# S5 tiles in a pool that gives way to gelu's, gelu in two halves, S5 transfers on POOL's queue: one change to a hybrid decoder layer

## The chip, the cores and the metric

One core of one Trainium2 chip. The metric is device time in microseconds of one execution.

## The reference, cut to what matters

A layer takes 320 token columns (256 of a prompt, 8 samples of 8) of width 2048. One projection feeds a convolution module and an S5 state-space layer; both are joined by an output projection, then come a SwiGLU FFN and a norm. All is fp32.

```python
def s5_mixer(u, h_re, h_im, A_re, A_im, log_dt, B_re, B_im, C_re, C_im, D, w_glu):
    ...
    bu_re = jnp.einsum('blgc,gpc->blgp', uf, Bb_re)
    bu_im = jnp.einsum('blgc,gpc->blgp', uf, Bb_im)
    ...
    _, _, hs_re, hs_im = lax.associative_scan(_complex_scan_op, (a_re, a_im, bu_re, bu_im), axis=1)
    y = (jnp.einsum('blgp,gcp->blgc', hs_re, C_re.astype(f32))
         - jnp.einsum('blgp,gcp->blgc', hs_im, C_im.astype(f32)))
    y = y + D.astype(f32).reshape(N_SSM_GROUPS, SSM_GROUP_CH) * uf
    y = jax.nn.gelu(y.reshape(b, l, D_SSM))
    y = y * jax.nn.sigmoid(y @ w_glu.astype(f32))
```

## The kernel before, in words

The weight matrices are read in slots: a slot is one raw tile of two blocks of 128 input rows by 512 columns (`run_slot`, L131). Its load is issued on SP's queue nine slots ahead (L116); ScalarE writes the high part hi (L126) and VectorE the rest lo (L127), two slots ahead; TensorE runs three products for each 128x128 block (L150 to L152). Every engine works through its own instructions strictly in order, and so does each queue of transfers, so a lo part that stands behind a waiting VectorE instruction holds up TensorE. The slots go: two groups for the S5 input (8 slots each), four for the convolution, then w_glu, w_out and the FFN (from about 450 us to the end).

Beside the projection's slots the S5 work is strewn in by the table PLAN (L31 to L45) and P_POST, P_CONV and P_GELU: each entry is a job and a slot number, its priority, from which a scheduler fixes the order in each engine's queue. There are eight blocks of 128 S5 channels. For each: `pool_v` (L602, tiles vw) and `pool_w` (L613, ww) multiply powers of the state matrix with B and C on VectorE; `s5_cblk` and `s5_pre` (L624, L631) make the kernel matrix ks; `kt_out` (L745) transposes it, adds D on a diagonal (dbc is D spread over the partitions by a transfer, dm that times a mask) and writes kt to KTd in DRAM (L756); `s_in_evac` (L656) puts the projected input into s_in and, after four blocks, sends it by eight transfers to ud in DRAM (L667) and by four back into us (L669); `s5_e`, `s5_scan` and `post` (L672, L703, L1154) make the states and the output yd, for which `make_t` (L758) reads tst from KTd. CT holds C transposed: its lower 64 partitions are written by ScalarE (L578), its upper 64 come from a tile up by a transfer (L582). `gelu` (L812) loads yd back as yl (L818, sixteen transfers) and needs the tiles ge and gehl, which lie where the pool s5 was; `open_g` (L794) closes that pool first. The convolution's `conv_chunk` (L342) fills ubuf (L361), spreads it by four transfers into ub (L371) and multiplies (L379). All of these transfers are on SP's queue.

```python
    def sm_tile(shape, name):
        return s5.tile(shape, F32, name=name, tag="sm", bufs=4)
```

dbc, dm, ks and kt share these four buffers.

Of the kernel before, what the change touches and what calls it, by code (L numbers as in the profile page):

```python
# [55 lines left out]
def kernel(ctx: ExitStack, tc: tile.TileContext,  # L56
# [208 lines left out]
    def channel_vectors():  # L265
        with when(13):
            p = sx_tile([128, 56])
            T.transpose(p, pvn, ident[:56, :56])
            V.tensor_copy(PV[:, 16:72], p)
            for h in range(2):  # L270
                ps = sx_tile([128, 4, 31])
                for c in range(4):
                    T.transpose(ps[:, c, :], late["cwn"][:31, (4 * h + c) * 128:(4 * h + c + 1) * 128],
                                ident[:31, :31])
                V.tensor_copy(convw[:, 4 * h:4 * h + 4, 0:31], ps)
# [10 lines left out]
    def rstd_bcast(dst, v):  # L286
# [3 lines left out]
        ps = sx_tile([128, NTOK])  # L290
        for j, (t0, n, _) in enumerate(tok):
            T.matmul(ps[:, t0:t0 + n], g[:n, j:j + 1].to_broadcast([n, 128]), ident[:n, :n],
                     start=True, stop=True)
        V.tensor_copy(dst, ps)
# [935 lines left out]
```

## Time and profile before

| what | us |
|---|---|
| median of 3 runs | 1442.85 (1442.59 to 1447.15) |
| profiled execution, its own time | 1442.68 |
| span of the profile | 1440.9 |
| TensorE busy | 1390.1 (96%) |
| VectorE busy | 793.9 (55%) |
| ScalarE busy | 550.2 (38%) |
| GpSimd (POOL) busy | 2.2 (17 instructions) |

The profile is one execution; the span leaves out a little at its ends. The page's chain that ended last is 84% TensorE, 6% transfers and 4% SP's queue. In the rows below PE is TensorE, DVE VectorE, ACT ScalarE, SP the queue of SyncE that issues transfers (SPq).

### The profile page before, as it was taken

How to read it: one execution, taken by the hardware profiler on the slowest of the kernel's cores; microseconds unless marked ns; L12 is line 12 of the kernel's file. 1: busy time of each engine (PE TensorE's matmuls, PEld its weight loads, DVE VectorE, ACT ScalarE, POOL GpSimd, SP SyncE). 2: the span in 40 equal slices, each digit the busy share in tenths (PEclk: the TensorE clock that was granted, in tenths of full speed). 3: DMA queues.
4: the chain of work that ended last, by engine and by line, in shares of the span. 5: the costliest groups of instructions: out<-in, count | busy, mean ns of one | idle time of the engine just before them, and what ended most of it. 6: DMA issues, size and time to landing. Idle time of an engine off the chain costs nothing.

```text
span 1440.9 us, 25146 instructions
## 1 busy us (share of the span) xinstructions
PE 1390.1 (96%) x10433; PEld 1358.5 (94%) x10433; DVE 793.9 (55%) x1408; ACT 550.2 (38%) x804; POOL 2.2 (0%) x17
## 2 busy tenths in 40 slices
PE   8899998989998999999999999999999999999995
PEld 7798978878998999999999999999999999999995
DVE  6677995354887845434544444344445444444465
ACT  7334433353454533333333332233333323333232
POOL 0000000000000000000000000000000000000000
PEclk9999998999999999999999999999999999999998
DMA  9775565596343444444444444444444454454432
GB/s 264 209 157 157 156 161 163 137 252 181 132 140 110 157 144 151 147 149 152 151 150 147 148 158 148 147 147 155 152 146 148 147 160 147 147 181 154 148 132 73
DMA packets 165579, 223.51 MB, mean 155 GB/s; under 512 B 40945, under 2 KB 77097, under 8 KB 165320
## 3 DMA queue, kind: packets, MB, share of 16 engines
q1 hardware_dynamic: 165464, 221.90, 50.9%
q8 instruction: 82, 1.34, 0.4%
q14 instruction: 33, 0.27, 0.1%
HBM read 201.56 MB, written 10.41 MB: 147 GB/s over the span
## 4 chain that ended last, share of the span: by engine, by line
PE 84%; DMA 6%; SPq 4%; DVE 3%; ACT 1%; issue 1%; ACTq 0%; DVEq 0%
PE mm L151 26%; PE mm L150 26%; PE mm L152 26%; DMA ub<-ubuf 2%; PE cx L379 2%; SPq L371 1%; SPq L667 1%; DMA raw<-in_w_in_dram 1%; DMA cn<-in_ssm_C_im_dram 1%; DVE lo L127 1%; PE sx L784 1%; DMA h<-xTd 1%; DMA ud<-s_in 0%; SPq L818 0%; PE sx L680 0%
## 5 line engine op out<-in xcount | busy, mean ns | idle before, releaser
L127 DVE TENSOR_TENSOR lo<-raw,hi 128x1024 fp32r<-128x1024 f32 x352 | 430.6, 1224 | 448.6 <-ACT hi L126 446.1
L126 ACT ACTIVATE hi<-raw 128x1024 fp32r<-128x1024 f32 x352 | 372.8, 1060 | 649.4 <-PE mm L151 580.7
L150 PE MATMUL mm<-hn,hi 128*128 128x320 f32 x1408 | 434.8, 309 | 0.0
L151 PE MATMUL mm<-hn,hi 128*128 128x320 f32 x1408 | 434.7, 309 | 0.0
L152 PE MATMUL mm<-hn,lo 128*128 128x320 f32 x1408 | 431.1, 309 | 0.0
L150 PEld LDWEIGHTS mm<-hn,hi 128*128 128x128 f32 x1408 | 264.3, 188 | 0.1
L151 PEld LDWEIGHTS mm<-hn,hi 128*128 128x128 f32 x1408 | 264.3, 188 | 0.0
L152 PEld LDWEIGHTS mm<-hn,lo 128*128 128x128 f32 x1408 | 263.2, 188 | 0.0
L150 PE MATMUL mm<-aout,hi 128*128 128x320 f32 x704 | 217.4, 309 | 0.0
L151 PE MATMUL mm<-aout,hi 128*128 128x320 f32 x704 | 217.1, 309 | 0.0
L152 PE MATMUL mm<-aout,lo 128*128 128x320 f32 x704 | 214.7, 309 | 0.0
L151 PEld LDWEIGHTS mm<-aout,hi 128*128 128x128 f32 x704 | 132.2, 188 | 0.0
L150 PEld LDWEIGHTS mm<-aout,hi 128*128 128x128 f32 x704 | 132.2, 188 | 0.0
L152 PEld LDWEIGHTS mm<-aout,lo 128*128 128x128 f32 x704 | 131.5, 188 | 0.0
L152 PE MATMUL mm<-xhl,lo 128*128 128x320 f32 x384 | 120.3, 318 | 5.7 <-DVE lo L127 5.7
L151 PE MATMUL mm<-xhl,hi 128*128 128x320 f32 x384 | 122.6, 321 | 0.5 <-DVE xhl L254 0.5
L150 PE MATMUL mm<-xhl,hi 128*128 128x320 f32 x384 | 118.0, 321 | 0.2 <-ACT xhl L253 0.2
L152 PEld LDWEIGHTS mm<-xhl,lo 128*128 128x128 f32 x384 | 73.8, 193 | 6.4 <-DVE lo L127 6.0
L151 PEld LDWEIGHTS mm<-xhl,hi 128*128 128x128 f32 x384 | 74.2, 193 | 1.9 <-DVE xhl L254 0.7
L150 PEld LDWEIGHTS mm<-xhl,hi 128*128 128x128 f32 x384 | 72.7, 193 | 1.6 <-issue 1.0
L1048 DVE TENSOR_TENSOR h<-mm,h 128x320 f32<-128x320 f32 x64 | 30.0, 488 | 41.1 <-PE mm L152 41.1
L379 PE MATMUL cx<-ub,cw 128*32 128x256 f32 x512 | 36.3, 391 | 9.4 <-DMA ub<-ubuf 9.4
(306 smaller groups left out, 1322.7 us busy)
## 6 DMA issues: line engine op xcount, KB each, us to landing
raw<-in_w_ffn_gate_dram SPq DMA_DIRECT2D x88, 512.0 KB
raw<-in_w_ffn_up_dram SPq DMA_DIRECT2D x88, 512.0 KB
raw<-in_w_ffn_down_dram SPq DMA_DIRECT2D x88, 512.0 KB
raw<-in_w_in_dram SPq DMA_DIRECT2D x64, 256.0 KB
raw<-in_w_out_dram SPq DMA_DIRECT2D x32, 512.0 KB
ub<-ubuf SPq DMA_DIRECT2D x32, 316.0 KB
raw<-in_w_in_dram SPq DMA_DIRECT2D x16, 512.0 KB
tst<-KTd SPq DMA_DIRECT2D x8, 512.0 KB
```

What stands on the lines that cost most here:

```text
L126: A.activation(hi, src, AF.Copy)
L127: V.tensor_tensor(lo, src, hi.bitcast(F32), op=OP.subtract)
L150: T.matmul(ps, wh, xh, start=(k == 0), stop=False)
L151: T.matmul(ps, wh, xl, start=False, stop=False)
L152: T.matmul(ps, wl, xh, start=False, stop=(k == g.nk - 1))
L371: SP.dma_start(ub[:, b, :], bass.AP(tensor=u.tensor, offset=u[32 * b:32 * b + 32].offset, ap=[[u.ap[0][0], 32], [8, 4], [1, UW - 24]]))
L379: T.matmul(acc[32 * b:32 * b + 32, 0:256], cw[:, b, k, :], ub[:, b, k:k + 256], start=(k == 0), stop=False, skip_group_check=True)
L667: SP.dma_start(o[g], s_in[16 * g:16 * g + 16].rearrange("c m s j -> c (m s) j"))
L784: T.matmul(ps[:, g, :], t2[:, g].rearrange("p t c -> p (t c)"), uall[:, 8 * b + g, :], start=False, stop=(g == 7), skip_group_check=True)
L1048: V.tensor_tensor(h[:, n, :], ps, h[:, n, :], op=OP.add)
```

## The change

It has five parts. (1) The tiles that the first half of the S5 work uses (s_in, cblk, vw, et, prm, tb, braw, cn0) lie in a pool s5v of their own; `open_ge` closes it early, and ge and yl take its place. (2) gelu's jobs are split: blocks 0 to 3 come four slots after the fourth post, blocks 4 to 7 after the last one, and the hi/lo parts are made by a job of their own, `gelu_parts`; one ScalarE step of gelu is folded into a VectorE one. P_POST moves by up to two slots. (3) CT's upper half is written directly: 32 matmuls to 64 rows in place of 16 transposes, and no transfer; cn1 has a buffer of its own. (4) D enters ks on VectorE by a constant matrix e7 and a column of the parameter table PV; dbc and dm are gone, and ks and kt alone share the four sm buffers. (5) The transfers to and from ud, KTd, and xTd into h are issued by GpSimd (`G.dma_start`). Small moves: the zero fill of KTd is one transfer, the parameter rows load earlier, and the conv taps have a function of their own.

```diff
--- before.py
+++ after.py
@@ -20,9 +20,8 @@
-P_POST = [24, 25.5, 27, 28.5, 30, 31.5, 33, 34.5]
+P_POST = [26 + 1.5 * b for b in range(8)]
...
-P_GELU = 44
@@ -38,8 +37,12 @@
+        + [("open_ge", 0, S1 + 4.5)]
+        + [("gelu", b, P_POST[3] + 4 + b) for b in range(4)]
...
-        + [("gelu", b, P_GELU + b / 2) for b in range(8)]
+        + [("gelu2", b, P_POST[7] + 1.2 + 0.1 * b) for b in range(4)]
+        + [x for b in range(4, 8) for x in (("gelu", b, P_POST[7] + 2 + 0.5 * b),
+                                            ("gelu2", b, P_POST[7] + 2.1 + 0.5 * b))]
@@ -159,10 +162,11 @@
-    dmask = const.tile([128, 16], F32, name="dmask")
+    dmask = tmp.tile([128, 8, 16], F32, tag="t", name="dmask")
...
-    V.tensor_scalar(dmask, im, 112.0, None, op0=OP.is_equal)
+    V.tensor_scalar(dmask, im[:, None, :].to_broadcast([128, 8, 16]), 112.0, None, op0=OP.is_equal)
+    e7 = const.tile([128, 128], F32, name="e7")
@@ -179,27 +183,29 @@
-               (gnorm_conv, 8), (gnorm_ssm, 8)]
-    PV = const.tile([128, 72], F32, name="PV")
+               (gnorm_conv, 8), (gnorm_ssm, 8), (ssm_D, 8)]
+    PV = const.tile([128, 80], F32, name="PV")
...
     def pv(i):
...
-    NMIX, NFFN, CB, LNG, LNB, GNC, GNS = 0, 16, 32, 40, 48, 56, 64
+    NMIX, NFFN, CB, LNG, LNB, GNC, GNS, SSD = 0, 16, 32, 40, 48, 56, 64, 72
...
+    vpool = ctx.enter_context(ExitStack())
+    s5v = vpool.enter_context(tc.tile_pool(name="s5v", bufs=1, side="right"))
...
     def sm_tile(shape, name):
...
-    pvn = tmp.tile([56, 128], F32, tag="t", name="pvn")
+    pvn = tmp.tile([64, 128], F32, tag="t", name="pvn")
@@ -229,6 +235,8 @@
+
+    def load_taps():
@@ -263,16 +271,20 @@
     def channel_vectors():
...
+        p = sx_tile([128, 64])
+        T.transpose(p, pvn, ident[:64, :64])
+        V.tensor_copy(PV[:, 16:80], p)
+        p = sx_tile([128, 128])
+        T.transpose(p, dmask.rearrange("p g c -> p (g c)"), ident)
+        A.activation(e7, p, AF.Copy)
+
+    def tap_vectors():
...
@@ -406,10 +419,10 @@
-    s_in = s5.tile([128, 4, 8, 41], F32, name="s_in")
+    s_in = s5v.tile([128, 4, 8, 41], F32, name="s_in")
...
-    Cblk = [s5.tile([128, 4, 2, 2, 16], F32, name=f"cblk{i}") for i in range(N_CBLK)]
+    Cblk = [s5v.tile([128, 4, 2, 2, 16], F32, name=f"cblk{i}") for i in range(N_CBLK)]
     def cmul(eng, outr, outi, ar, ai, br, bi, t1, t2):
@@ -441,8 +454,9 @@
     def s5_load2():
-        braw = s5.tile([128, 2, 32, 16], F32, tag="et", name="braw", bufs=ET)
-        cn = [s5.tile([128, 8, 64], F32, name=f"cn{i}", tag="et", bufs=ET) for i in range(2)]
+        braw = s5v.tile([128, 2, 32, 16], F32, tag="et", name="braw", bufs=ET)
+        cn = [s5v.tile([128, 8, 64], F32, name="cn0", tag="et", bufs=ET),
+              s5.tile([128, 8, 64], F32, name="cn1", tag="ww", bufs=VW)]
@@ -556,30 +570,31 @@
         G.memset(hbd, 0.0)
-        for b in range(8):
-            SP.dma_start(KTd[b, 8:15], z)
+        SP.dma_start(KTd[:, 8:15].rearrange("b s c n -> (s c) b n"),
+                     z[:, None, :].to_broadcast([112, 8, 128]))
...
         kib = kim[:, :, None].to_broadcast([128, 32, 16])
-        tb = s5.tile([128, 2, 512], F32, name="tb", tag="vw", bufs=VW)
+        tb = s5v.tile([128, 2, 512], F32, name="tb", tag="vw", bufs=VW)
...
-        up = s5.tile([64, 2, 32, 16], F32, name="up", tag="ww", bufs=VW)
...
             for h in range(2):
-                ps = sx_tile([64, 4, 128])
+                ps = sx_tile([128, 4, 128])
                 for k in range(4):
-                    T.transpose(ps[:, k, :], cn[r][:, 4 * h + k, :], ident)
-                for g2, dst in enumerate((CT[:64], up)):
-                    A.activation(dst[:, r, 16 * h:16 * h + 16, :]
+                    for g2 in range(2):
+                        T.matmul(ps[64 * g2:64 * g2 + 64, k, :], cn[r][:, 4 * h + k, :], ident,
+                                 start=True, stop=True)
+                for g2 in range(2):
+                    sl = slice(64 * g2, 64 * g2 + 64)
+                    A.activation(CT[sl, r, 16 * h:16 * h + 16, :]
                                  .rearrange("p (k q) c -> p k q c", k=4),
-                                 ps.rearrange("p k (q g c) -> p k q g c", q=4, g=2)[:, :, :, g2, :],
+                                 ps[sl].rearrange("p k (q g c) -> p k q g c", q=4, g=2)[:, :, :, g2, :],
                                  AF.Copy, scale=-1.0 if r else 1.0)
-        SP.dma_start(CT[64:128], up)
@@ -650,7 +665,7 @@
-        A.activation(ks, ps, AF.Copy)
+        V.scalar_tensor_tensor(ks, e7, pv(SSD + b), ps, op0=OP.mult, op1=OP.add)
...
     def s_in_evac(b, ps):
@@ -664,9 +679,9 @@
         for g in range(8):
-            SP.dma_start(o[g], s_in[16 * g:16 * g + 16].rearrange("c m s j -> c (m s) j"))
+            G.dma_start(o[g], s_in[16 * g:16 * g + 16].rearrange("c m s j -> c (m s) j"))
         for m in range(b - 3, b + 1):
-            SP.dma_start(uall[:, 8 * m:8 * m + 8, :].rearrange("p g j -> p (g j)"),
+            G.dma_start(uall[:, 8 * m:8 * m + 8, :].rearrange("p g j -> p (g j)"),
...
     def s5_e(b):
@@ -743,21 +758,15 @@
     def kt_out(b, ks):
-        dbc = sm_tile([128, 128], "dbc")
-        SP.dma_start(dbc, bass.AP(tensor=ssm_D.tensor, offset=ssm_D.offset + 128 * b,
-                                  ap=[[0, 128], [1, 128]]))
-        dm = sm_tile([128, 8, 16], "dm")
-        V.tensor_tensor(dm, dbc.rearrange("p (g c) -> p g c", g=8),
-                        dmask[:, None, :].to_broadcast([128, 8, 16]), op=OP.mult)
...
         kt = sm_tile([128, 128], "kt")
-        V.tensor_tensor(kt, ps, dm.rearrange("p g c -> p (g c)"), op=OP.add)
-        SP.dma_start(KTd[b, 0:8], kt)
+        A.activation(kt, ps, AF.Copy)
+        G.dma_start(KTd[b, 0:8], kt)
     def make_t(b):
         ts_ = s5.tile([128, 8, 8, 16], F32, name="tst", tag="tst", bufs=1)
-        SP.dma_start(ts_, bass.AP(tensor=KTd.tensor, offset=KTd.offset + b * 15 * 2048,
+        G.dma_start(ts_, bass.AP(tensor=KTd.tensor, offset=KTd.offset + b * 15 * 2048,
@@ -791,12 +800,17 @@
+    def open_ge():
+        vpool.close()
+        gst = cpool.enter_context(ExitStack())
+        late["gep"] = gst.enter_context(tc.tile_pool(name="gep", bufs=1, side="right"))
+        late["ge"] = late["gep"].tile([128, 8, NTOK], F32, name="ge")
+
     def open_g():
...
-        late["ge"] = gp.tile([128, 8, NTOK], F32, name="ge")
...
     def open_mid():
@@ -810,23 +824,27 @@
     def gelu(b):
-        gp = late["gp"]
-        ge, gehl = late["ge"], late["gehl"]
+
+        gep, ge = late["gep"], late["ge"]
         if b % 4 == 0:
-            yls = late["yl"] = gp.tile([128, 32, 40], F32, name="yl", bufs=2)
+            yls = late["yl"] = gep.tile([128, 32, 40], F32, name="yl", bufs=2)
...
         yl = late["yl"][:, 8 * (b % 4):8 * (b % 4) + 8]
-        sq = gp.tile([128, 8, 40], F32, name="gsq", bufs=3)
-        A.activation(sq, yl, AF.Square)
-        A.activation(sq, sq, AF.Copy, bias=C0, scale=C0 * 0.044715)
-        z = gp.tile([128, 8, 40], F32, name="gz", bufs=3)
-        V.tensor_tensor(z, sq, yl, op=OP.mult)
-        A.activation(z, z, AF.Sigmoid)
+        if b < 4:
+            z = s5.tile([128, 8, 40], F32, name="gz", tag="pt1", bufs=PT_BUFS)
+        else:
+            z = late["gp"].tile([128, 8, 40], F32, name="gz", bufs=3)
+        A.activation(z, yl, AF.Square)
+        V.scalar_tensor_tensor(z, z, 1.0 / 0.044715, yl, op0=OP.add, op1=OP.mult)
+        A.activation(z, z, AF.Sigmoid, scale=C0 * 0.044715)
...
         V.tensor_tensor(gv, z, yl, op=OP.mult)
+
+    def gelu_parts(b):
+        ge, gehl = late["ge"], late["gehl"]
@@ -945,8 +963,8 @@
-            A.activation(h[:, k, 0:1], late["ge"][:, 4, 0:1], AF.Copy)
-            SP.dma_start(h[:, k:k + 4, :], xTd[:, k:k + 4, :])
+            A.activation(h[:, k, 0:1], late["ssm"][:, 0, 7 if k else 3, 0:1].bitcast(F32), AF.Copy)
+            G.dma_start(h[:, k:k + 4, :], xTd[:, k:k + 4, :])
     def m1_done(i, R):
         def f(m, ps):
@@ -1124,6 +1142,7 @@
+        load_params()
@@ -1135,8 +1154,11 @@
-        load_params()
-    channel_vectors()
+        load_taps()
+    with when(2):
+        channel_vectors()
+    with when(13):
+        tap_vectors()
@@ -1157,9 +1179,9 @@
-    parts_ = dict(v=pool_v, pre=pre, e=s5_e, w=pool_w, scan=s5_scan, post=post, gelu=gelu,
+    parts_ = dict(v=pool_v, pre=pre, e=s5_e, w=pool_w, scan=s5_scan, post=post, gelu=gelu, gelu2=gelu_parts,
...
-                  states=lambda b: s5_states(), open_g=lambda b: open_g(),
+                  states=lambda b: s5_states(), open_g=lambda b: open_g(), open_ge=lambda b: open_ge(),
...
```

**SP's queue where the first S5 input is sent.** Names are tile<-source; raw is a weight load. Before:

```order
L116 DMA raw<-in_w_in_dram 128x2x512
L233 DMA cwn<-in_conv_w_dram 31x1024
L667 DMA ud<-s_in 16x32x41 x8
L582 DMA CT<-up 64x1024
L116 DMA raw<-in_w_in_dram 128x2x512
L669 DMA us<-ud 128x328 x4
L116 DMA raw<-in_w_in_dram 128x2x512
L116 DMA raw<-in_w_in_dram 128x2x256 x8
L336 DMA tapd<-convw 128x8x32
L337 DMA tapw<-tapd 128x32x8
L116 DMA raw<-in_w_in_dram 128x2x256 x3
```

The change:

```order
L119 DMA raw<-in_w_in_dram 128x2x512 x3
L119 DMA raw<-in_w_in_dram 128x2x256 x8
L349 DMA tapd<-convw 128x8x32
L119 DMA raw<-in_w_in_dram 128x2x256 x2
L350 DMA tapw<-tapd 128x32x8
L119 DMA raw<-in_w_in_dram 128x2x256 x38
```

The eight ud, four us, CT and dbc rows are no longer between the weight loads.

**POOL's queue, the change.** Before it held no transfer.

```order
L682 DMA ud<-s_in 16x32x41 x8
L684 DMA us<-ud 128x328 x4
L765 DMA KTd<-kt 128x128
L682 DMA ud<-s_in 16x32x41 x8
L765 DMA KTd<-kt 128x128
L684 DMA us<-ud 128x328 x4
L765 DMA KTd<-kt 128x128 x3
L769 DMA tst<-KTd 128x8x128
L765 DMA KTd<-kt 128x128
L769 DMA tst<-KTd 128x8x128
L765 DMA KTd<-kt 128x128 x2
L769 DMA tst<-KTd 128x8x128 x6
```

The KTd row of block 1 stands behind the second eight ud rows, each tst row behind the KTd rows ahead of it.

**SP's queue around gelu's loads.** so and uo are outputs, stn the convolution's old state. Before:

```order
L818 DMA yl<-yd 16x32x40
L116 DMA raw<-in_w_glu_dram 128x2x512
L818 DMA yl<-yd 16x32x40 x6
L116 DMA raw<-in_w_glu_dram 128x2x512
L818 DMA yl<-yd 16x32x40 x9
L353 DMA stn<-in_state_conv_dram 120x2x128
L371 DMA ub<-ubuf_110 128x1x632 x4
```

The change, the first eight yl rows:

```order
L832 DMA yl<-yd 16x32x40 x3
L384 DMA ub<-ubuf_114 128x1x632 x4
L832 DMA yl<-yd 16x32x40
L799 DMA yd<-y_2682 128x320
L379 DMA out_dram<-uo 30x128
L380 DMA out_dram<-uo 8x8x128
L119 DMA raw<-in_w_in_dram 128x2x256 x2
L832 DMA yl<-yd 16x32x40 x4
```

And the second eight:

```order
L832 DMA yl<-yd 16x32x40
L747 DMA out_dram<-so_3142 32x128
L747 DMA out_dram<-so_3147 32x128
L832 DMA yl<-yd 16x32x40 x5
L119 DMA raw<-in_w_in_dram 128x2x256 x2
L756 DMA out_dram<-so_3154 8x16x128
L832 DMA yl<-yd 16x32x40 x2
L756 DMA out_dram<-so_3161 8x16x128
```

Eight of the sixteen now stand behind the yd row of block 3, among the S5 outputs; the other eight stand among the state outputs, and the next chunk's stn and ub come behind them.

## Rows read from the trace of the kernel before

**Rows 1.** Windows: time; busy of PE, PEld, DVE, ACT, POOL; PEclk; DMA; GB/s.
```profile
60.00:120.00 60.00, 51.26 (x361) 48.44 (x360) 37.46 (x74) 19.73 (x30) 0.00 (x0) 0.91 0.79 172
...
280.00:360.00 80.00, 68.94 (x940) 62.49 (x940) 41.20 (x64) 36.26 (x79) 0.00 (x0) 0.98 0.84 216
...
450.00:1400.00 950.00, 950.00 (x6480) 949.75 (x6480) 456.31 (x596) 336.61 (x393) 0.00 (x0) 1.00 0.47 150
```

**Rows 2.** Windows of 20 us, same columns.
```profile
60.00:80.00 20.00, 14.26 (x80) 12.95 (x79) 10.13 (x29) 4.86 (x6) 0.00 (x0) 0.83 0.82 198
100.00:120.00 20.00, 17.01 (x132) 16.14 (x131) 11.04 (x17) 7.46 (x13) 0.00 (x0) 0.91 0.98 195
...
280.00:300.00 20.00, 14.42 (x185) 12.88 (x185) 7.35 (x11) 7.70 (x19) 0.00 (x0) 0.91 1.07 183
```

**Rows 3.** Waits of TensorE, 0 to 500 us: total us, times, longest.
```profile
PE cx L379 <- DMA ub<-ubuf: 9.4, 8, 2.0
PE mm L152 <- DVE lo L127: 6.7, 2, 5.7
PE sx L363 <- ACT ubuf L361: 4.8, 1, 4.8
PE sx L650 <- DVE kt L755: 3.0, 1, 3.0
...
PE sx L576 <- DMA cn<-in_ssm_C_im_dram: 1.4, 1, 1.4
```

**Rows 4.** Timeline of VectorE: start, us, instruction, idle before and releaser.
```profile
70.67 0.69 DVE L595 TENSOR_TENSOR ww<-pw,CT 128x512 f32<-128x512 f32 x1 [9.87 <-DMA CT<-up]
...
111.02 0.29 DVE L750 TENSOR_TENSOR dm<-dbc,dmask 128x128 f32<-128x128 f32 x1 [6.32 <-DMA dbc<-in_ssm_D_dram]
```

**Rows 5.** Timeline of SP's queue, 44 to 76 us: start, us, issue.
```profile
53.55 11.44 SPq L667 DMA_DIRECT2D ud<-s_in  x8
65.09 0.63 SPq L582 DMA_DIRECT2D CT<-up  x1
```

**Rows 6.** Timeline of SP's queue, 90 to 135 us.
```profile
95.55 4.17 SPq L667 DMA_DIRECT2D ud<-s_in  x6
99.82 0.65 SPq L756 DMA_DIRECT2D KTd<-kt  x1
...
106.86 0.35 SPq L747 DMA_DIRECT2D dbc<-in_ssm_D_dram  x1
...
130.15 0.34 SPq L756 DMA_DIRECT2D KTd<-kt  x1
```

**Rows 7.** Timeline of SP's queue, 276 to 300 us.
```profile
281.81 6.33 SPq L818 DMA_DIRECT2D yl<-yd  x6
...
288.72 6.03 SPq L818 DMA_DIRECT2D yl<-yd  x9
```

**Rows 8.** Timeline of ScalarE, 280 to 300 us.
```profile
293.79 0.47 ACT L823 ACTIVATE gsq<-yl 128x320 f32<-128x320 f32 x1 [7.75 <-DMA yl<-yd]
294.17 0.35 ACT L361 ACTIVATE ubuf<-sx 128x240 f32<-128x240 f32 x1
```

**Rows 9.** Groups of TensorE by shape, 40 to 130 us: busy us, mean ns.
```profile
L650 PE MATMUL sx<-vw,cblk 128*32 128x128 f32 x64 | 2.7, 279 | 3.0 <-DVE kt L755 3.0
L576 PE MATMUL sx<-ident,cn 128*64 128x128 f32 x16 | 2.2, 272 | 1.4 <-DMA cn<-in_ssm_C_im_dram 1.4
```

**Rows 10.** Single lines, L667 and L760: ns min/median/max, first and last start.
```profile
L667 SPq DMA_DIRECT2D ud<-s_in x16: 331/770/4909, 53.6 to 101.9; - x16
...
L760 SPq DMA_DIRECT2D tst<-KTd x8: 360/368/1667, 153.7 to 245.8; - x8
```

**Rows 11.** Groups of VectorE, 45 to 125 us: busy us, mean ns, idle before.
```profile
L275 DVE COPY convw<-sx 128x124 f32<-128x124 f32 x2 | 0.6, 286 | 0.4 <-PE sx L273 0.4
```

More of the change, by code (lines that the diff above doesn't have):

```diff
@@ L257, in x_block @@
                 nc.any.tensor_copy(xr, ps)
-            with when(k):
+            with when(k / 2 - 1):
                 SP.dma_start(xTd[:, k, :], xr)
@@ L265, in channel_vectors @@
     def channel_vectors():
[L266 to L275, printed above, removed]
+        p = sx_tile([128, 64])
[5 more added lines that the diff above has]
+    def tap_vectors():
+        for h in range(2):
+            ps = sx_tile([128, 4, 31])
+            for c in range(4):
+                T.transpose(ps[:, c, :], late["cwn"][:31, (4 * h + c) * 128:(4 * h + c + 1) * 128],
+                            ident[:31, :31])
+            V.tensor_copy(convw[:, 4 * h:4 * h + 4, 0:31], ps)
     def newton_rsqrt(dst, v, t):
@@ L284, in newton_rsqrt, with rstd_bcast @@
             V.scalar_tensor_tensor(dst, t, 1.5, dst, op0=OP.add, op1=OP.mult)
-    def rstd_bcast(dst, v):
+    def rstd_bcast(dst, v, later=0):
         g, t = (tmp.tile([128, 3], F32, name=n, tag="rt", bufs=4) for n in ("rg", "rt"))
         newton_rsqrt(g, v, t)
[L290 to L294, printed above, removed]
+        with when((tc.cur_priority - BASE) / SLOT + later):
+            ps = sx_tile([128, NTOK])
+            for j, (t0, n, _) in enumerate(tok):
+                T.matmul(ps[:, t0:t0 + n], g[:n, j:j + 1].to_broadcast([n, 128]), ident[:n, :n],
+                         start=True, stop=True)
+            V.tensor_copy(dst, ps)
     def token_mean(src, n_ch):
@@ L466, in s5_params @@
             T.transpose(ps[:, i, :], dtn if i == 2 else an[i], ident[:32, :32])
-        prm = s5.tile([128, 1024], F32, name="prm", tag="vw", bufs=VW)
+        prm = s5v.tile([128, 1024], F32, name="prm", tag="vw", bufs=VW)
         P = s5p["P"] = prm[:, 0:512].rearrange("p (i q) -> p i q", q=32)
@@ L569, in s5_params2 @@
         cmul(V, Bb[:, 0], Bb[:, 1], krb, kib, braw[:, 0], braw[:, 1], tb0, tb1)
-        up = s5.tile([64, 2, 32, 16], F32, name="up", tag="ww", bufs=VW)
         for r in range(2):
             for h in range(2):
-                ps = sx_tile([64, 4, 128])
+                ps = sx_tile([128, 4, 128])
                 for k in range(4):
-                    T.transpose(ps[:, k, :], cn[r][:, 4 * h + k, :], ident)
-                for g2, dst in enumerate((CT[:64], up)):
-                    A.activation(dst[:, r, 16 * h:16 * h + 16, :]
+                    for g2 in range(2):
+                        T.matmul(ps[64 * g2:64 * g2 + 64, k, :], cn[r][:, 4 * h + k, :], ident,
+                                 start=True, stop=True)
+                for g2 in range(2):
+                    sl = slice(64 * g2, 64 * g2 + 64)
+                    A.activation(CT[sl, r, 16 * h:16 * h + 16, :]
                                  .rearrange("p (k q) c -> p k q c", k=4),
-                                 ps.rearrange("p k (q g c) -> p k q g c", q=4, g=2)[:, :, :, g2, :],
+                                 ps[sl].rearrange("p k (q g c) -> p k q g c", q=4, g=2)[:, :, :, g2, :],
                                  AF.Copy, scale=-1.0 if r else 1.0)
-        SP.dma_start(CT[64:128], up)
         for r in range(2):
@@ L602, in pool_v @@
     def pool_v(b):
-        v = s5.tile([128, 4, 2, 8, 16], F32, name="vw", tag="vw", bufs=VW)
+        v = s5v.tile([128, 4, 2, 8, 16], F32, name="vw", tag="vw", bufs=VW)
         Vt[b] = v
@@ L637, in s5_pre @@
         else:
-            e = s5.tile([128, 4, 2, 128], F32, name="et", tag="et", bufs=ET)
+            e = s5v.tile([128, 4, 2, 128], F32, name="et", tag="et", bufs=ET)
         Et[b] = e
@@ L852, in rms @@
     def rms(src, n, dst):
-        rstd_bcast(dst, token_mean(src, n))
+        rstd_bcast(dst, token_mean(src, n), later=1)
     ln = {}
```

## The prediction

> **What bounds the kernel now.** I read the busy times by stage first. From 450 to 1400 us TensorE is busy 950.00 of 950 us at the full granted clock [rows 1]: the FFN is dense, and nothing in the change touches it or the order of TensorE's work behind the gelu section. So the change can only win where TensorE stands still earlier, and before 450 us there is little: 8.7 us in 60 to 120, 11.1 us in 280 to 360 [rows 1]. Cut finer, three stretches of 20 us hold most of what the change speaks of: 60 to 80 (14.26 busy, granted clock .83), 100 to 120 (17.01, .91) and 280 to 300 (14.42, .91) [rows 2]. [...] In a stretch whose clock is .91, about 9% of 20 us is lost to that, 1.8; I take 1.7 for each stall, a little less because some of the slow time falls into the stall itself.
>
> Second, TensorE's waits. One of 5.7 us on the lo part of a weight tile, one of 4.8 on ScalarE's copy into ubuf, one of 3.0 on kt; the ub waits are eight and spread (9.4 us in all, longest 2.0) [rows 3]. The engine named in the first is only a messenger: VectorE's queue stood 9.9 us before ww, for the transfer CT<-up, and 6.3 us at the longest before dm, for the transfer dbc [rows 4]. Its lo parts are queued behind. So I read the DMA queue. On SP the first eight ud transfers take 11.44 us to issue, and CT<-up, next in the row, starts at 65.09 [rows 5]; VectorE goes on at 70.67, which is 5.6 us of issue and landing. In the second half the last two ud's and the raw loads stand ahead of dbc, which issues at 106.86 [rows 6] and releases VectorE at 111.02, 4.2 us later [rows 4]. The third stall is also SP's: yl x6 takes 6.33 us and yl x9 6.03 [rows 7], ScalarE stands 7.75 us before its first square of yl [rows 8], and the ubuf copy that TensorE waits for is right behind that square in ScalarE's queue.
>
> **The change part by part.** *CT without a transfer.* The upper half of CT comes from TensorE and the row CT<-up goes. VectorE's 9.9 us and TensorE's 5.7 go with it: idle 20 − 14.26 = 5.7 [rows 2] plus 1.7 of clock, **−7.4**. What is late next is cn's imaginary part, for which TensorE already waited 1.4 us [rows 3]; with a buffer of its own it is issued right behind the real part, so I expect no new wait there. The price: 32 plain matmuls to 64 rows in place of 16 transposes. The transposes took 2.2 us, 0.137 each; 64 plain matmuls to 32 rows took 2.7 us, 0.042 each with four side by side [rows 9]. Two side by side would be 0.084, 32 of them 2.7, that is +0.5; none side by side, at the 279 ns that one lasts, 8.9, that is +6.7. I take the transposes' own rate, 4.4 for 32: **+2.2**, since their shape is nearest.
>
> *The D term without a transfer.* dbc and dm go, so their wait goes: idle 3.0 [rows 2, 3] plus 1.7, **−4.7**. The added product of e7 with D is one VectorE instruction of the shape that dm had, kt's sum becomes a copy on ScalarE, and the zero fill and the early parameter loads change queues that nothing waits on then: 0. One more transpose for e7: +0.3 (0.137 by [rows 9], doubled for its copy).
>
> *Gelu in two halves.* The first eight yl transfers and gelu 0 to 3 move ahead, beside the S5 outputs. The 5.6 us idle at 280 to 300 plus 1.7 make 7.3 at most. The second eight yl's stay on SP, at their old place ahead of gelu 4 to 7; the row of nine took 6.03 [rows 7], so about half the issue is left, and it no longer comes after another half. Bounds 0 and −7.3; I take **−5**. What is late next is ub, whose eight waits stay.
>
> *S5 transfers on POOL's queue.* 44 transfers leave SP: 16 ud, 8 us, 8 KTd, 8 tst, 4 h. SP's gain is counted in the three terms above. POOL has nothing to do in these stretches [rows 1], but the trace has no DMA of POOL's, so the price of an issue there is unknown. The nearest rows are SP's own ud's: 331 ns the shortest, 770 the median, 4909 the longest [rows 10]. I take 11.44 / 8 = 1.4 us, the first burst's mean, as the eight come in a burst on POOL too. What waits behind them: KTd of block 1 stands behind the second eight ud's, and with only two buffers of each kind kt of block 3 cannot be written before it has landed; ScalarE's hi parts queue behind that kt. The time it has: kt 3 went out at 130.15, the second burst began at 95.55 [rows 6], less 4.7 for the removed stall is 29.9; less 4.2 for a landing like dbc's and 0.4 for its issue, 25.3, or **3.2 us for each ud**. At 1.4 it is hidden: 0. The first burst's readers come far later.
>
> Sum: −7.4 + 2.2 − 4.7 + 0.3 − 5 = −14.6. The profiled execution took 1442.68 us, in the middle of the runs shown (median 1442.85). **Forecast 1428 us.** With both ends of the terms: CT's matmuls at +0.5 and yl at −7.3 give 1424; at +6.7 and 0 they give 1437.6. The low end I put at 1418, because moving 44 issues away from SP may also shorten waits that I left at their old size (the ub waits, 9.4).
>
> [...] What the rows show is that VectorE, while POOL would be issuing, runs almost nothing but tensor-tensor operations: the costliest group from 45 to 125 us that isn't one is a pair of copies of 0.6 us [rows 11], read from PSUM. [...] No row before shows a POOL transfer beside VectorE.
>
> **The rivals.** *B, POOL's queue becomes the bound (slower).* Issue on POOL grows with the number of pieces (512 in a ud, 1024 in a tst), and eight in a row block KTd of block 1. Above 3.2 us per ud each further microsecond costs 8. The tst's, at twice the pieces, come every (245.8 − 153.7) / 7 = 13.2 us [rows 10]; with one buffer, twice the ud's time plus 4.2 of landing must fit, which ends at 4.5 us. At 4.9: 8 × 1.7 = 13.6, tst 7 × (9.8 + 4.2 − 13.2) = 5.6, and eight more stalls with their slow clock 8 × 1.7 = 13.6; +32.8 − 14.6 gives 1461. It turns to slower near **4.5 us**. For it: the one row of 4909 ns, and that nothing of POOL is known. Against: on SP the median is 0.77, and tst with twice the pieces has a median of 0.37 [rows 10], so issue isn't priced by pieces there. Chance 0.18.
>
> *L, POOL issues only while VectorE stands.* From 100 to 120 us VectorE is busy 11.04 of 20 us [rows 2], so POOL has 45%: from 95.5 to the limit at 120.8 that is 11.4 us. Eight ud's at 1.4 just fit (1428); at twice that, 22.9, 11.5 are missing, a stall that with its clock makes +13.2: 1441. For it: no row speaks. [...] Chance 0.05.
>
> *C, the gain goes into new waits.* CT's matmuls at +6.7, yl at 0 because its second half still stands ahead of the ubuf copy, and ub's landing waits half again as long (+4.7): 1442.7 − 7.4 + 6.7 − 4.7 + 0.3 + 4.7 = 1442. For it: TensorE's order is dense, and a wait removed tends to be met by the next. Against: after 9.9 us of VectorE's wait no other transfer is shown late there. Chance 0.12.
>
> **How the numbers follow.** Forecast 0.65, B 0.18, C 0.12, L 0.05. A measurement of this kernel can tell about 0.3%, 4.3 us, from no change: faster is under 1438.5, slower over 1447.2. The forecast is faster, C and L lie between, B is slower: 0.65, 0.17, 0.18. The range, 1418 to 1452, holds the forecast with its bounds, C, L and the beginning of B; left out are most of B (0.13) and a gain beyond the terms (0.05).
>
> **What would show it.** Right: no wait on CT before ww, and no dm; TensorE over 18.5 busy in the 20 us that follow the first S5 slots and again around the second ud burst; no wait of 4.8 us on L361's counterpart; POOL's ud's under 3.2 us each; the FFN stretch as long as before. Wrong, by B: KTd of block 1 issued over 25 us behind the burst's start and ScalarE waiting for it before a kt; by L: ud issues that grow where VectorE is busy; by C: TensorE's waits on ub and the ubuf copy above 14.2 us in all. Slower with all POOL issues under 3 us would leave my reasoning without a cause.

## The result and the profile after

The changed kernel takes 1435.36 us (median of 6 runs, 1431.72 to 1438.16), the kernel before 1443.36 in the runs beside it: ratio 0.9944, 95% interval 0.992 to 0.9967. That is faster by 8 us, about half of the 14.6 forecast. Two stalls went as forecast, one moved, and one came that the prediction does not have.

The windows of the changed kernel (columns as in [rows 1]):

```profile
0.00:60.00 60.00, 54.86 (x347) 49.44 (x349) 44.13 (x166) 35.41 (x78) 4.81 (x21) 0.94 0.91 260
60.00:120.00 60.00, 60.00 (x514) 56.34 (x511) 47.16 (x92) 26.86 (x46) 14.01 (x25) 1.00 0.81 174
120.00:280.00 160.00, 149.02 (x1565) 130.87 (x1562) 117.63 (x278) 67.07 (x141) 9.37 (x12) 0.93 0.56 150
280.00:360.00 80.00, 74.73 (x892) 69.59 (x892) 41.94 (x61) 33.58 (x64) 0.56 (x1) 1.00 0.62 176
...
450.00:1400.00 950.00, 950.00 (x6485) 949.74 (x6484) 454.57 (x593) 334.93 (x390) 0.00 (x0) 1.00 0.47 151
```

From 60 to 120 TensorE is now busy 60.00 of 60 us at a granted clock of 1.00 (51.26 and .91 before, [rows 1]). The FFN is as it was. But the first stretch shows a granted clock of 0.94 where it had 1.00, and the third has 149.02 busy and 0.93, where the kernel before had 153.51 and 0.96. In windows of 20 us, the same columns:

```profile
40.00:60.00 20.00, 17.94 (x134) 16.45 (x134) 15.15 (x42) 6.73 (x12) 2.66 (x4) 0.91 0.85 267
60.00:80.00 20.00, 20.00 (x144) 18.34 (x141) 17.52 (x46) 8.85 (x14) 4.67 (x9) 1.00 0.94 194
...
100.00:120.00 20.00, 20.00 (x210) 18.79 (x209) 14.91 (x22) 9.78 (x19) 4.28 (x8) 1.00 0.93 208
...
220.00:240.00 20.00, 15.65 (x95) 10.59 (x93) 8.52 (x18) 6.15 (x12) 1.77 (x2) 0.70 0.76 185
240.00:260.00 20.00, 19.50 (x197) 15.59 (x200) 7.77 (x11) 6.52 (x17) 0.00 (x0) 0.79 0.41 99
260.00:280.00 20.00, 16.28 (x183) 13.66 (x175) 7.57 (x15) 8.26 (x22) 0.00 (x0) 0.91 0.68 140
280.00:300.00 20.00, 19.73 (x232) 18.50 (x232) 12.43 (x17) 9.29 (x18) 0.00 (x0) 1.00 0.71 182
```

60 to 80, 100 to 120 and 280 to 300 answer to [rows 2]: 20.00, 20.00 and 19.73 busy in place of 14.26, 17.01 and 14.42. The loss now lies from 220 to 280 and from 40 to 60, where the kernel before had:

```profile
40.00:60.00 20.00, 18.59 (x129) 17.60 (x128) 17.78 (x47) 9.30 (x20) 0.00 (x0) 1.00 0.86 262
...
220.00:240.00 20.00, 16.31 (x185) 14.98 (x185) 16.93 (x44) 6.45 (x13) 0.00 (x0) 0.74 0.41 126
240.00:260.00 20.00, 19.19 (x166) 15.68 (x168) 2.16 (x3) 6.54 (x15) 0.00 (x0) 0.91 0.60 152
260.00:280.00 20.00, 20.00 (x203) 19.11 (x195) 8.62 (x11) 8.34 (x17) 0.00 (x0) 1.00 0.53 134
```

TensorE's waits in the changed kernel, as in [rows 3]:

```profile
PE cx L392 <- DMA ub<-ubuf: 12.4, 8, 4.4
PE sx L753 <- ACT stg L751: 3.7, 2, 2.9
PE mm L153 <- ACT hi L129: 2.1, 1, 2.1
```

The waits on ubuf, kt and cn are gone, and of those on lo 1.0 us is left of 6.7. ub's eight waits grew from 9.4 to 12.4, the longest from 2.0 to 4.4, and waits on ScalarE, for the outgoing states (stg, L751) and for a weight part (hi), are new.

Where each microsecond changed hands is best read from when the same work begins. The table has the start of the first product with a lo part (L152, now L155) of some weight slots, read from the traces of one execution each:

| slot | before | after | difference | what lies between |
|---|---|---|---|---|
| 8 | 49.09 | 54.32 | +5.2 | a weight load that lands late, ScalarE waits 4.5 us for it |
| 14 | 82.93 | 82.43 | -0.5 | CT: 5.7 won |
| 24 | 136.79 | 131.62 | -5.2 | D: 4.7 won |
| 32 | 171.95 | 166.22 | -5.7 | |
| 44 | 288.13 | 293.35 | +5.2 | S5 outputs, gelu 0 to 3: 11.0 lost |
| 46 | 302.11 | 300.50 | -1.6 | the old yl stall: 6.8 won |
| 60 | 377.57 | 370.91 | -6.7 | convolution's end: 5.1 won |
| 130 | 638.03 | 630.89 | -7.1 | |

S5 and convolution work is moved between slots 32 and 60, so only the whole of that stretch compares: 205.6 us before, 204.7 after, 0.9 won where gelu's term said 5. A second pair of traces (experiments 8 and 5) gives +4.9 up to slot 8, 8.4 won from 8 to 14, 6.2 won from 14 to 24, and 0.9 lost from 32 to 60: the same picture, with up to 2.7 us between two executions of one kernel in these stretches. Of the 5.2 us at slot 8, 1.4 stand at slot 2 already, less than the 2.08 between the two traces of the kernel before.

POOL's queue, as single lines (ns min/median/max) and in its timeline:

```profile
L682 POOL DMA_DIRECT2D ud<-s_in x16: 628/628/789, 57.3 to 99.9; - x16
```
```profile
L769 POOL DMA_DIRECT2D tst<-KTd x8: 882/898/923, 141.9 to 229.3; - x8
```
```profile
220.25 0.88 POOL L769 DMA_DIRECT2D tst<-KTd  x1 [4.83 <-ACT t L772]
...
340.30 0.56 POOL L967 DMA_DIRECT2D h<-xTd  x1 [110.15 <-DVE lo L130]
```

A ud issue takes 0.63 us and never more than 0.79, a tst of twice the pieces 0.90: far under the 3.2 and 4.5 us from which rival B decides. VectorE was busy 47.16 of the 60 us in which most of them ran.

### The profile page after: what moved, and what is told of

Its sections match the earlier page's. It is cut to its first block, busy times and chain, and to the rows that moved or that the text cites. A ratio compares the mean times of both kernels' runs of the same rounds, so it can differ in the third digit from the quotient of the medians.

```text
span 1433.6 us, 25240 instructions
## 1 busy us (share of the span) xinstructions
PE 1393.3 (97%) x10482; PEld 1358.0 (95%) x10482; DVE 794.0 (55%) x1400; ACT 550.9 (38%) x797; POOL 30.4 (2%) x61
## 4 chain that ended last, share of the span: by engine, by line
PE 87%; DMA 5%; DVE 4%; SPq 2%; ACT 1%; issue 1%; ACTq 0%; DVEq 0%
PE mm L154 27%; PE mm L153 27%; PE mm L155 27%; DMA ub<-ubuf 3%; PE cx L392 2%; SPq L384 1%; DMA raw<-in_w_in_dram 1%; DVE us L711 1%; DVE lo L130 1%; DMA out_dram<-so 1%; PE sx L695 1%; SPq L119 0%; PE cx L396 0%; DVE scw L708 0%; DVE scw L707 0%
## 5 line engine op out<-in xcount | busy, mean ns | idle before, releaser
L155 PE MATMUL mm<-hn,lo 128*128 128x320 f32 x1408 | 431.1, 309 | 0.0
L155 PEld LDWEIGHTS mm<-hn,lo 128*128 128x128 f32 x1408 | 263.2, 188 | 0.0
L155 PE MATMUL mm<-aout,lo 128*128 128x320 f32 x704 | 214.7, 309 | 0.0
L155 PEld LDWEIGHTS mm<-aout,lo 128*128 128x128 f32 x704 | 131.5, 188 | 0.0
L155 PE MATMUL mm<-xhl,lo 128*128 128x320 f32 x384 | 120.9, 318 | 0.0
L155 PEld LDWEIGHTS mm<-xhl,lo 128*128 128x128 f32 x384 | 73.6, 192 | 1.1 <-issue 0.6
L392 PE MATMUL cx<-ub,cw 128*32 128x256 f32 x512 | 38.3, 412 | 12.4 <-DMA ub<-ubuf 12.4
```

The lines of the kernel that those rows point to most:

```text
L155: T.matmul(ps, wl, xh, start=False, stop=(k == g.nk - 1))
L392: T.matmul(acc[32 * b:32 * b + 32, 0:256], cw[:, b, k, :], ub[:, b, k:k + 256], start=(k == 0), stop=False, skip_group_check=True)
```

## The experiments

Each ratio is to the kernel before, run beside it on the same chip; times of different groups (runs 1 to 4, 5 to 8, 9 to 11, 12) are not compared directly, since the kernel before took 1448.67, 1446.95, 1444.57 and 1443.35 in them.

One thing limits the comparisons. The scheduler fixes each engine's order anew for every version. In the traces the changed kernel (experiment 5 too) and experiment 7, all with tst on POOL's queue, have the same order on TensorE, VectorE and ScalarE, instruction for instruction. Experiments 1, 6, 10 and 11, with tst on SP's, share a second order, which differs from the first between about 150 and 285 us. Experiments 2, 3, 9 and 12 each have one of their own. So what tst's queue does is never seen without another order, and what the queue of the other four kinds does is seen with the order unchanged: changed kernel against 7, and 6 against 1.

**1. Everything back on SP's queue.**

```diff
-        G.dma_start(...)
+        SP.dma_start(...)
```

> All 44 transfers that the change gave to POOL are issued on SP's queue again; the rest of the change stays. Theory A (the two transfers CT<-up and dbc were the loss, not the queue): no VectorE instruction waits for a transfer behind the ud burst any more, so TensorE keeps at least 59 us busy in 60 to 120, and the time stays within 3 us of the changed kernel, 1433 to 1438. Rival B (the eight ud issues on SP, 11.44 us in a row, were the loss): the weight loads behind the burst come late, ScalarE's hi parts wait for them, TensorE loses 4 us or more again near 60 to 80 or 100 to 120, and the time is 1440 to 1446.

Measured: 1425.99 us, ratio 0.985 (0.9825 to 0.9874), better than either theory said. TensorE is busy 60.00 of 60 us from 60 to 120, so theory A is right that the two transfers, not the burst of ud issues (6.26 us here), were the loss. But the move to POOL does not cost nothing: the version without it is faster, though in another order of the engines. The difference arises between slots 32 and 60 (190.8 us against 204.7), 6.3 us of it before slot 40, which covers 220 to 260 us. First the changed kernel, SP's issue of ub and TensorE's wait for it (start, us, instruction, idle before):

```profile
217.94 5.12 SPq L384 DMA_DIRECT2D ub<-ubuf  x4
```
```profile
229.27 2.78 PE L392 MATMUL cx<-ub,cw 128*32 128x256 f32 x20 [4.35 <-DMA ub<-ubuf]
```

Then the version on SP: windows, SP's queue, and TensorE at the same place.

```profile
220.00:240.00 20.00, 16.94 (x151) 13.29 (x150) 11.57 (x25) 6.65 (x15) 0.00 (x0) 0.91 0.79 179
240.00:260.00 20.00, 16.63 (x267) 13.67 (x267) 6.18 (x9) 8.18 (x21) 0.00 (x0) 1.00 0.73 168
```
```profile
218.98 5.11 SPq L384 DMA_DIRECT2D ub<-ubuf  x4
...
231.49 2.15 SPq L769 DMA_DIRECT2D tst<-KTd  x1
```
```profile
228.64 2.38 PE L392 MATMUL cx<-ub,cw 128*32 128x256 f32 x20 [2.42 <-DMA ub<-ubuf]
```

On POOL tst goes out at 220.25, amid the issue of ub; on SP it stands behind ub and yl and goes out at 231.49. ub is then waited for 2.42 us instead of 4.35, and the granted clock is .91 and 1.00 in the 40 us from 220 on instead of .70 and .79.

**2. yl on POOL's queue too.**

```diff
-                SP.dma_start(yls[16 * g:16 * g + 16],
+                G.dma_start(yls[16 * g:16 * g + 16],
```

> The changed kernel with gelu's sixteen yl loads on POOL's queue too. Theory A (the split moved gelu's jam on SP's queue to the S5 outputs, where yl stands ahead of ub): the wait for ub of 4.4 us falls to 2 or less, the granted clock of 0.70 from 220 to 240 rises, time 1428 to 1432. Rival B (the slow clock there comes of the small matmuls of the S5 outputs and the convolution standing together, whatever the queue): the wait shrinks but the clock from 220 to 250 stays under 0.8, time 1433 to 1437.

Measured: 1432.12 us, ratio 0.9888 (0.987 to 0.9906). The wait for ub stayed (4.84 us) and the clock from 220 to 240 was .75, so A's cause is wrong although the time improved; the scheduler also put weight products among the S5 outputs, so the run settles nothing more.

**3. gelu in one piece, POOL kept.**

```diff
-        + [("gelu", b, P_POST[3] + 4 + b) for b in range(4)]
...
+        + [x for b in range(8) for x in (("gelu", b, 44 + 0.5 * b), ("gelu2", b, 44.1 + 0.5 * b))]
```

> The changed kernel with gelu in one piece at its old slots (44 to 47.5), all sixteen yl loads together on SP again. Theory A (the split gained next to nothing in the end: the stall at 280 to 300 went, an equal one came at 220 to 270): time within 2 us of the changed kernel, 1433 to 1438, a wait of 4 us or more on yl back, and less lost from 220 to 270. Rival B (the split is worth the 5 us of the prediction and something else costs): 1439 to 1443.

Measured: 1431.98 us, ratio 0.9896 (0.9868 to 0.9924). Neither: it lies below the changed kernel's 0.9944 and 0.9934 (the intervals just touch), and no wait on yl of 4 us came back. With S5's transfers on POOL's queue the split wins nothing. And with gelu in one piece POOL's queue shows no cost in time: 0.9896 here, 0.9919 with everything on SP (experiment 9), intervals overlapping. The loss is seen only where the split and the move stand together.

**4. CT alone, on the kernel before.**

```diff
-        SP.dma_start(CT[64:128], up)
...
+                        T.matmul(ps[64 * g2:64 * g2 + 64, k, :], cn[r][:, 4 * h + k, :], ident,
```

> The kernel before, with nothing changed but CT's upper half written by matmuls to 64 rows, without the transfer up. Theory A (the transfer CT<-up alone held VectorE): the 9.9 us wait of VectorE and the 5.7 of TensorE go; time 5 us under the kernel before, 1436 to 1440. Rival B (what stands behind the ud burst on SP is late anyway): the next wait, on a weight load, takes the place; TensorE under 17 us busy in the 20 us from 60 on, time within 2 us of the kernel before, 1441 to 1446.

Measured: 1450.37 us, ratio 1.0015 (0.9999 to 1.0031): no gain, though TensorE was busy 20.00 of the 20 us from 60 on. Against the kernel before on the same kind of run (experiment 8) it reaches slot 8 at 56.18 instead of 51.17, slot 14 at 83.89 instead of 87.67, slot 24 at 143.13 instead of 143.05. So 8.8 us are won between slots 8 and 14, and 5.0 are given back ahead of them and 3.9 behind, where dbc still stands. Its waits of TensorE:

```profile
PE sx L651 <- DVE kt L756: 4.7, 1, 4.7
...
PE sx L292 <- ACT convy L257: 3.5, 1, 3.5
```

The first row stands in experiment 8 too, with the same 4.7, so it isn't what was given back; three waits of 1.1 to 1.3 us on VectorE (vw, s_in, lo) that experiment 8 doesn't have come to 3.5. The second row is the giving back ahead: there ScalarE waited 7.38 us for an xTd store to land. From about 39 us on SP's queue too has another order than in the kernel before.

**5. The changed kernel again.**

> The changed kernel once more, word for word, as the yardstick for the runs beside it on the same chip. Theory A: it is faster than the kernel before by 0.4 to 0.8%, and in its profile the wait for ub of about 4 us near 229 us and the low granted clock behind it stand again. Rival: both belonged to the one profiled execution, and the clock from 220 to 250 us is above 0.9.

Measured: 1438.03 us, ratio 0.9934 (0.9919 to 0.9949). Theory A: the wait for ub was 5.04 us, the clock .73 and .76 from 220 to 260.

**6 and 7. Only tst back on SP; only tst on POOL.**

```diff
-        G.dma_start(ts_, ...
+        SP.dma_start(ts_, ...
```

That is the edit of 6; 7 is experiment 1 with the same line turned round (SP to G).

> The changed kernel with the eight tst loads alone back on SP's queue; ud, us, KTd and h stay on POOL's. Theory A (on POOL's queue a tst load of 1024 pieces goes out while ub is being issued and takes its bandwidth; on SP it stands behind ub): as fast as the version with everything on SP, 8 us or more under the changed kernel, no wait for ub over 2.6 us between 220 and 240 and a granted clock of 0.9 or more there. Rival B (the ud transfers on POOL's queue are what costs): within 3 us of the changed kernel.

> The reverse of the run before it: everything on SP's queue but the eight tst loads, which stay on POOL's. Theory A: the changed kernel's slow stretch from 224 to 248 us is there, time within 3 us of the changed kernel. Rival B: as fast as the version with everything on SP, 8 us or more under the changed kernel.

Measured: 0.989 (0.9874 to 0.9906) with tst alone on SP, 0.9876 (0.9841 to 0.9911) with tst alone on POOL, 0.9934 with all on POOL. Theory A holds for the wait: 2.52 us with tst on SP, 4.36 with tst on POOL,

```profile
229.95 2.77 PE L392 MATMUL cx<-ub,cw 128*32 128x256 f32 x20 [2.52 <-DMA ub<-ubuf]
```
```profile
229.58 2.77 PE L392 MATMUL cx<-ub,cw 128*32 128x256 f32 x20 [4.36 <-DMA ub<-ubuf]
```

and for the slow stretch, which was there with tst on POOL (.71 and .78). In time it does not carry the loss alone: with tst alone on SP the clock from 220 to 240 was still .70, and with tst alone on POOL the kernel gained as much as with tst alone on SP (the intervals overlap). How late ub lands can be read in all versions, from the end of its issue to TensorE's first product with it: for this third chunk 6.2 to 8.3 us in the five traces with tst on POOL (changed kernel, 2, 3, 5, 7), 4.2 to 5.0 in the five with tst on SP whose wait ended with ub (1, 6, 9, 10, 12). So tst beside ub makes ub land about 2 us later; what that costs is not separated from the other order.

The move of ud, us, KTd and h is separated: against experiment 5, in the same order, experiment 7 is 8 us faster (0.9876 to 0.9934, intervals apart). A part of it is h, which stayed on POOL in 6 and not in 7. The convolution's last wait for ub, first with h on POOL (and its issue), then on SP:

```profile
334.54 0.54 POOL L967 DMA_DIRECT2D h<-xTd  x1 [158.06 <-DMA ub<-ubuf]
```
```profile
342.82 5.35 PE L392 MATMUL cx<-ub,cw 128*32 128x256 f32 x64 [3.10 <-DMA ub<-ubuf]
```
```profile
343.18 3.67 PE L392 MATMUL cx<-ub,cw 128*32 128x256 f32 x64 [0.62 <-DMA ub<-ubuf]
```

3.10 us against 0.62; in the changed kernel 3.03, with h issued at 340.30 (above), in the version on SP 0.44. From the end of ub's issue it took 7.0 to 7.9 us in the five traces with h on POOL (changed kernel, 2, 3, 5, 6), 4.85 to 5.36 in the six with h on SP (1, 7, 9, 10, 11, 12). Slots 46 to 60, where all but experiment 2 have the same order, took 69.2 to 71.1 us with h on POOL and 66.8 to 68.7 on SP. No run moved h alone, but it is the only S5 transfer on POOL's queue behind 230 us: about 3 us are its.

**8. The kernel before again.**

> The kernel before once more, for a profile on the same chip. Between weight slots 6 and 8 the changed kernel lost 4 us against the kernel before, by a late weight load, though the loads there are nearly the same. Theory A (a matter of the chip and the execution, since the version with CT alone showed it too): this profile shows a loss of 3 us or more there as well. Rival B (the change's own earlier loads cause it): it shows none, and reaches slot 8 within 1 us of 49.1 us.

Measured: 1447.81 us (one run). It is 2.08 us late at slot 2 and still 2.08 late at slot 8, so it loses nothing between slots 6 and 8; the changed kernel beside it (experiment 5) loses 5.2 there. That is rival B's side, though slot 8 came at 51.17 and not within 1 us of 49.1: the change brings that loss. That its earlier loads do isn't shown, since experiment 4, which has none of them, loses 5.3 between the same slots, behind another wait.

**9. gelu in one piece, everything on SP.**

The edit is that of experiment 3, made to the kernel of experiment 1.

> Everything on SP's queue and gelu in one piece at its old slots, the rest of the change kept. With POOL's queue in use the one piece was faster than the split. Theory A (the split costs wherever the transfers are issued: its first half adds work and yl loads to the crowded stretch of the S5 outputs): ratio to the kernel before 0.983 or less, the stretch from 220 to 260 us shorter than with the split, and no wait of 4 us on yl later. Rival B (the split only hurt because tst on POOL's queue had already delayed ub; on SP it earns its 5 us): ratio 0.988 or more, with a wait on yl of 4 us or more between 270 and 300.

Measured: 1432.08 us, ratio 0.9919 (0.9891 to 0.9947), against 1426 to 1427 for experiments 10 and 11 beside it, which have the split. Rival B's size is right: on SP's queue the split earns 5 to 6 us, by intervals that still overlap. Its sign is not: no wait on yl, but these, and a clock of .85 from 240 to 260.

```profile
PE cx L389 <- DMA ub<-ubuf: 8.6, 7, 3.1
PE sx L750 <- ACT stg L748: 2.8, 1, 2.8
...
PE sx L790 <- ACT t L769: 1.7, 1, 1.7
```

**10 and 11. The copy of 704 KB left out; cn1 one weight load later.**

```diff
-        + [("copy", 0, 65)])
+        )
...
+        with when(5):
+            SP.dma_start(cn[1], ssm_C_im[0] ...
```

> Everything on SP's queue, and the copy of 704 KB from the old convolution state to the new one left out: part of the output new_conv_sample, rows 0 to 21, is not written. The order on the engines stays the same. Theory A (that copy, issued half a microsecond behind a weight load, takes its bandwidth: the load of slot 8 takes 7 to 9 us to land): ScalarE's wait of 4 to 6 us for that load falls under 2, slot 8 comes 3 us or more earlier, and the ratio falls to 0.983 or less. Rival B (the loads of B and C ahead of it, in small pieces, hold it): slot 8 moves by under 1 us, ratio 0.984 to 0.987.

> Everything on SP's queue, and the load of C's imaginary part (cn1) moved behind one more weight load, where the change had put it right behind the real part. Theory A (cn1 so early delays the weight load of slot 8): slot 8 comes 2 us or more earlier than 55.8 us, ratio 0.983 to 0.984. Rival B (that load is held by something else): slot 8 within 1 us of 55.8, ratio 0.984 to 0.987.

Measured: 1426.96 us, 0.9885 (0.9855 to 0.9916), and 1426.01 us, 0.9873 (0.9842 to 0.9904). Slot 8 came at 55.83 and 54.65, where experiment 1 had 55.78. The copy is not the cause; cn1 is at most 1.1 of the 5 us.

**12. Parameter loads back in their old place.**

```diff
-        load_params()
...
+        load_params()
...
-    with when(2):
+    with when(4.5):
```

> Everything on SP's queue, and the eight small parameter loads and their transposes moved back to the place that the loads had before (slot 4, the transposes at 4.5), so that a weight load stands between the loads of B and those of C again. Theory A (the early loss of 5 us before slot 8 comes from a weight load pushed behind the loads of C in small pieces): slot 8 comes at 52.5 us or earlier instead of 55.8, the ratio is 0.983 or less. Rival B (the transfers of that stretch fill it whatever their order, and another one becomes late): slot 8 within 1.5 us of 55.8, ratio 0.984 to 0.988. Rival C (the parameters now come late for the D term): VectorE or TensorE waits for them before slot 12 and the ratio is above 0.988.

Measured: 1428.67 us, 0.9892 (0.9872 to 0.9912). A weight load stood ahead of C's loads again, and slot 8 came at 56.92. Another load was late: ScalarE's waits from 26 to 60 us, first the changed kernel, then this one.

```profile
ACT hi L129 <- DMA raw<-in_w_in_dram: 4.5, 1, 4.5
```
```profile
ACT hi L129 <- DMA raw<-in_w_in_dram: 9.4, 2, 7.9
```

Theory A falls. What makes a weight load late before slot 8 stays open; that it is a load, in a stretch whose transfers fill 0.91 of the DMA engines' time (0 to 60 us; before the change too), is shown. All versions that lose there have CT's new form, experiment 4 included; none was run without it.

## Why the prediction was right or wrong

The sign was right, and 1435.36 lies in the range, which is 34 us wide. The point, 1428, was 7 us too low. The signs of being right that the prediction named all came (no wait on CT or dbc, 20.00 busy in both stretches, no wait of 4.8 us on ubuf, issues under 3.2 us), and none of them tests the terms that failed. By the table the sum came out as -5.7 (CT), -4.7 (D), -0.9 (slots 32 to 60), +5.2 (ahead of slot 8) and about -1 in between and behind: -7.1 at slot 130, where -14.6 was forecast.

The 1.7 us of slow clock in three of the terms was my estimate from the .91 of [rows 2]; no run shows it apart from its stall. In windows of 2 us the trace of the kernel before is near it: from 70 to 76 us, behind the first stall, TensorE is busy 3.45 us at a granted clock of 0.50 to 0.52, and half of that is 1.7. After the change the three stretches of 20 us have a clock of 1.00.

*CT*: forecast -7.4 for the stall and +2.2 for the matmuls. The stall went whole; 5.7 us were won from slot 8 to 14, and that is net of the matmuls, so it answers to -7.4 + 2.2 = -5.2. The matmuls took 3.9 us where the transposes took 2.2, so +1.7:

```profile
L590 PE MATMUL sx<-ident,cn 128*64 128x128 f32 x64 | 3.9, 276 | 0.0
```

The 4.4 us for all 32 at the transposes' rate were near, but by luck: the trace has two records for each of these matmuls (64 for 32), and the records start in pairs, 7 ns apart, with 109 ns from most pairs to the next; twice the records, two side by side, cancel. Read with two records each, L650's 64 in [rows 9] are 32 matmuls at 0.084 us, and the lower bound of +0.5 would have been +3.2.

*D*: forecast -4.7, measured 4.7 from slot 14 to 24. That both were messengers' waits, and the transfer behind them the cause, is confirmed by experiment 1, where they stay away with the ud burst back on SP. In the kernel before, ScalarE had written a hi part by 60.83 us, and the lo part made from it began only at 71.27, when ww, ahead of it on VectorE, had run (70.67 to 71.36).

*Gelu in two halves*: forecast -5. The old stall went (6.8 won), but a like loss came up at 220 to 270, 0.9 in all. On SP's queue the split is worth 5 to 6 us (experiments 9 to 11, intervals overlapping), so the term was about right for itself and wrong beside the next one.

*S5 transfers on POOL's queue*: this step failed. I priced the issue, bounded it well (0.63 us, under the 1.4 taken), and put 0, since it was hidden. What I left out is what an earlier issue does to others: tst, free of its place behind ub, goes out beside it, and ub lands about 2 us later (6.2 to 8.3 us from the end of its issue, against 4.2 to 5.0); so does the last chunk's ub beside h (7.0 to 7.9 against 4.85 to 5.36), where about 3 us are lost. With every transfer on SP the ratio is 0.985, 0.9873 and 0.9892 (experiments 1, 11, 12), with all five kinds on POOL 0.9944 and 0.9934: 6 to 14 us, beside the split; with gelu in one piece no such cost is seen (experiments 3 and 9). ud, us, KTd and h account for 8 us with the engines' order unchanged (experiment 7 against 5), h for about 3 of them; what the other 5 are stays open. tst's own share isn't settled, since every version with tst on SP has another order. Rival C named the place, ub's landing waits, but priced it at 4.7 without the clock, and for another cause.

The wait for ub was 4.35, 5.04 and 4.36 us with tst on POOL (the changed kernel, experiments 5 and 7), 2.42 and 2.52 with it on SP (1 and 6).

*The small moves ahead of slot 8*, put at 0 because nothing waited on their queues: 5 us were lost there. The stretch was full of transfers already (a DMA share of 0.91 from 0 to 60 us, before the change too), and any of four orders of the loads kept a weight load late. The cause is open, and so whether these moves or CT's new form bring it.

Rival L did not come. Of the 16 ud issues on POOL 13 ran wholly while VectorE was busy and took 628 to 789 ns; the one during which VectorE stood, at 60.63 us, took 628. What VectorE ran beside them were tensor-tensor operations, but for one copy (beside the issue at 59.39 us) and one scalar-tensor-tensor operation (97.38); these two issues took 628 ns too.

## What to carry to other kernels

When transfers leave a crowded queue, price not only the issue but what they will meet when they go out earlier: a place behind a critical transfer may be worth more than a free queue. With tst behind ub TensorE waited 2.52 us for ub, with tst beside it 4.36 (experiments 6 and 7, in different orders of the engines). After a queue change, see first whether the engines' order is still the same; where it isn't, the queue alone was not tried. A removed wait can be given back elsewhere: experiment 4 won 8.8 us between slots 8 and 14 and gave back 5.0 ahead of them and 3.9 behind. So compare the start of the same work in both traces, stage by stage, before adding up gains. The best version here keeps CT, D and the split and issues everything on SP: ratio 0.985 in its group, and 0.9873 with cn1 a little later.
